# Neighbourhood attention and gated DeltaNet in one layer: keys, queries and values moved ahead of the gates, and the inverse's merges in a pool of their own

## The chip, the cores and the metric

The kernel runs on one core of one Trainium2 chip. The metric is the device time of one execution in microseconds (us). Before the change three runs gave 906.75, 904.99 and 906.35, a median of 906.35 us. The engines are called as in the profile: PE is TensorE (matrix products), PEld its weight load, DVE VectorE, ACT ScalarE, POOL GpSimd and SP SyncE, which issues nearly all DMAs. Each works through its own instructions in order.

## The reference

One layer mixes 1024 latent tokens (width 1024) and reads 256 context tokens. One input projection feeds two groups of heads; both are gated, joined and projected back:

```
h  = rmsnorm(x, g_pre) * (1 + scale) + shift          # modulated by c; hc for the context
na_q, na_k, na_v, na_z, g_qkv, g_z, g_b, g_a = split(h @ w_in)
o_na = neighborhood_attention(na_q, na_k, na_v, na_kc, na_vc, rpb)   # 8 heads of 64
q, k, v = gdn_qkv(g_qkv, conv_w)                       # short conv + silu, l2norm, rope; 4 heads of 128
...
a     = where(pos[:, None] > pos[None, :], (k * beta) @ k.T * decay, 0)
t_inv = inverse(eye + a)                               # one triangular inverse per chunk and direction
u, w  = t_inv @ (v * beta), t_inv @ (k * beta * exp(gc))
scan over chunks: v_new = u - w @ state; o = q_dec @ state + qk @ v_new; state = ...
...
y   = concat(o_na * silu(na_z), rmsnorm(o_g) * silu(g_z)) @ w_out
out = x + gate * rmsnorm(y, g_post)
```

DeltaNet runs in both directions. The kernel takes chunks of 128 tokens, so that there are ten blocks of 128 x 128 per head and direction (eight latent, two of context) whose triangular inverse is wanted.

## The kernel before

Five stages follow one another. **Setup and phase 0** load the modulation, form `h` and `hc` as pairs of a high and a low part (`hh`, `hl`), and make the first products. **Phase 2** runs over the four DeltaNet heads: per head the convolved projections of q and k, the front of the previous head (`delta_front`, which makes the triangular matrices `pm` and writes them to `pm_dram`), v, the token-wise work of q and k. **Phase a2** finishes the inverses. **Phase b** is neighbourhood attention (NA) with the scans of the DeltaNet heads woven in. **Phase 4** is the output projection.

Each product of float32 accuracy is three products: high by high, low by high, high by low (L460, L464, L465). Projections that nothing needs before phase b (NA's keys, queries, values and gates, and the gates of DeltaNet heads 1 to 3) are given out in steps by one generator, `projections` (L778). Phase 2 takes one step at each letter `p` of a string:

```
for c in "RVppTppUB":
    step(h, c)
    next(blocks, None)
```

That is four steps per head, sixteen in all. What is left of the generator is used up in phase a2. A step is one gate half (24 products of 512 columns), one block of keys or queries (24 of 512, or of 256 for the context), or values of two token tiles. `na_proj` writes keys and queries to `qk_dram` through `qk_out`; `gate_proj` writes gates to `z_dram`.

**The inverse** of a 128 x 128 block goes in two steps. The 32 x 32 diagonal blocks are inverted by substitution on DVE (`inv_blocks`, L1003 and L1006), in three groups: merge 0 needs group 0, merge 1 groups 0 and 1, merge 2 group 1, merge 3 group 2. Groups 0 and 1 run within phase 2, group 2 in phase a2 (generator `blocks`). The results go to `yd`. Then `inv_merge` (L1014), once per head, builds the 64 x 64 and then the 128 x 128 inverse from them: `vd` is the inverted diagonal blocks, loaded back, `ld` their transposes, `pmf` the head's `pm` matrices (two loads of 640 KB), `tz` the first products (PSUM), `zt` their copy in SBUF, `tu` the second products, which DVE scales by -1 into `tm` or `xo`; `tz2`, `z2`, `tu2` are the same at 64 x 64. The finished `tm` goes to `tm_dram`. The diagonal blocks are copied into `tm` and `xo` by twelve ACT copies. The trace prints `tz2` and `tu2` as `tz` and `tu`, without the head's number.

In phase a2 two generators, `blocks` and `merges`, are advanced beside the remaining projection steps, by a credit each. A Tile scheduler with a timeline of its own then sets the order of the instructions on every engine, by dependences and priority (`high_priority`); the merges run at a raised priority. The PSUM pool of these stages has three tags: `ta` (3 banks), `tb` (2) and `pj` (3).

## Time and profile before

| | |
|---|---|
| median of three runs | 906.35 us |
| profiled execution | 904.01 us, its span 902.3 us |
| mean granted PE clock | 0.963 |
| busy PE / DVE / ACT / POOL | 848.5 / 537.6 / 416.2 / 369.6 us |
| convolutions end (last key product of head 3) | 447.7 us |
| first merge product / first product of attention | 468.6 / 554.2 us |
| last stretch, the output projection, from about | 800 us |

The page gives busy time by engine, then forty slices of the span (each digit is tenths busy, for `PEclk` tenths of the full clock), then queues, the chain that ended last, and groups of instructions. A row of a timeline reads: start, length, engine, line, operation, output <- inputs, shape, count, and in brackets the idle time ahead of it with what ended it. A row of waits reads: engine, waiting tile and line, what it waited for, total us, times, longest. A row of DMA issues ends with the time from issue to landing. A row of a table of stretches reads: from:to, length, busy us (instructions) of PE, PEld, DVE, ACT and POOL, granted clock, share of the DMA engines, GB/s.

### The profile page before, as it was taken

How to read it: one execution, taken by the hardware profiler on the slowest of the kernel's cores; microseconds unless marked ns; L12 is line 12 of the kernel's file. 1: busy time of each engine (PE TensorE's matmuls, PEld its weight loads, DVE VectorE, ACT ScalarE, POOL GpSimd, SP SyncE). 2: the span in 40 equal slices, each digit the busy share in tenths (PEclk: the TensorE clock that was granted, in tenths of full speed). 3: DMA queues.
4: the chain of work that ended last, by engine and by line, in shares of the span. 5: the costliest groups of instructions: out<-in, count | busy, mean ns of one | idle time of the engine just before them, and what ended most of it. 6: DMA issues, size and time to landing. Idle time of an engine off the chain costs nothing.

```text
span 902.3 us, 16602 instructions
## 1 busy us (share of the span) xinstructions
PE 848.5 (94%) x6082; PEld 708.7 (79%) x6082; DVE 537.6 (60%) x1179; ACT 416.2 (46%) x1165; POOL 369.6 (41%) x431
## 2 busy tenths in 40 slices
PE   6999999999999989998998998999999988998996
PEld 4688887887788767787887877888887876887785
DVE  3463454456545699689428634677777775662442
ACT  5262525545645445652334444555545656532310
POOL 1432322614543532455241124568557569423210
PEclk9999999999999989999998985999999998999898
DMA  9786432346355534733799699949387152132351
GB/s 343 257 290 228 150 107 74 114 157 199 89 198 185 138 122 151 216 99 112 249 265 265 219 281 413 267 117 296 141 208 272 48 183 76 47 117 94 108 183 60
DMA packets 95176, 160.98 MB, mean 178 GB/s; under 512 B 28581, under 2 KB 55542, under 8 KB 92918
## 3 DMA queue, kind: packets, MB, share of 16 engines
q1 hardware_dynamic: 87606, 146.25, 51.2%
q10 hardware_dynamic: 7488, 13.67, 4.9%
q8 instruction: 48, 0.79, 0.4%
q14 instruction: 34, 0.28, 0.1%
HBM read 110.82 MB, written 52.42 MB: 181 GB/s over the span
## 4 chain that ended last, share of the span: by engine, by line
PE 64%; DVE 13%; DMA 9%; ACT 5%; issue 4%; POOL 2%; SPq 2%; ACTq 0%; DVEq 0%; POOLq 0%
PE py L1218 3%; PE py L1219 3%; PE py L1220 3%; DVE tb L1003 3%; PE pl L688 2%; DVE vb L1006 2%; PE po L715 2%; PE pl L697 2%; PE pz L464 2%; PE pc L684 2%; PE pz L460 2%; PE pz L465 2%; PE po L710 2%; PE pa L1138 2%; PE pa L1144 2%
## 5 line engine op out<-in xcount | busy, mean ns | idle before, releaser
L676 POOL TENSOR_TENSOR gm<-gt,mk 128x288 f32<-128x288 f32 (+1 forms) x64 | 64.3, 1009 | 36.0 <-DVE nm L693 35.9
L1125 POOL TENSOR_SCALAR kd<-kt,kd 128x128 f32<-128x128 f32 x72 | 43.4, 606 | 35.3 <-PE pa L1144 33.7
L694 ACT ACTIVATE pt<-pt,nm 128x288 f32<-128x288 f32 (+1 forms) x64 | 36.7, 574 | 35.7 <-DVE nm L693 35.5
L945 ACT ACTIVATE em<-em,gc 128x128 f32<-128x128 f32 x80 | 25.5, 391 | 38.2 <-DMA em<-gc_dram 32.3
L693 DVE CUSTOM_DVE_ANT_0 pt<-pl,gm,mi 128x288 f32<-128x288 f32 (+1 forms) x64 | 36.1, 564 | 11.5 <-PE pl L688 4.9
L699 DVE COPY tl<-pl 96x384 f32<-96x384 f32 (+1 forms) x64 | 35.3, 551 | 10.2 <-PE pl L697 9.9
L692 DVE TENSOR_REDUCE mi<-pc 128x1 f32<-128x256 f32 x64 | 26.8, 420 | 22.0 <-PE pc L684 21.1
L464 PE MATMUL pz<-hl,wh_gz 128*128 128x512 f32 x96 | 38.6, 402 | 0.0
L460 PE MATMUL pz<-hh,wh_gz 128*128 128x512 f32 x96 | 38.4, 400 | 0.0
L465 PE MATMUL pz<-hh,wl_gz 128*128 128x512 f32 x96 | 38.3, 399 | 0.0
L473 PE MATMUL pv<-wh_nv,hh 128*128 128x264 f32 x128 | 35.5, 295 | 2.5 <-ACT hh L262 1.7
L964 POOL TENSOR_SCALAR_AFFINE_SELECT qe<-qe 128x256 f32<-128x256 f32 x32 | 26.9, 840 | 25.8 <-DVE qe L963 25.8
L475 PE MATMUL pv<-wl_nv,hh 128*128 128x264 f32 x128 | 35.7, 286 | 1.5 <-POOL wl_nv L446 1.5
L474 PE MATMUL pv<-wh_nv,hl 128*128 128x264 f32 x128 | 36.5, 289 | 0.0
L1003 DVE TENSOR_TENSOR tb<-ab,vb 120x31 f32<-120x31 f32 (+15 forms) x62 | 32.1, 518 | 6.8 <-DMA ab<-ab_dram 5.1
L960 DVE SCALAR_TENSOR_TENSOR pm<-pk,beta,em 128x128 f32<-128x128 f32 x80 | 23.6, 343 | 19.9 <-PE pk L953 12.3
L697 PE MATMUL pl<-c,pt 128*96 128x128 f32 (+1 forms) x192 | 33.7, 285 | 1.4 <-ACT pt L694 1.2
L812 DVE SCALAR_TENSOR_TENSOR acc_v<-xp_v,cols,acc_v 128x1282 f32<-128x1282 f32 x16 | 27.5, 1719 | 9.0 <-ACT acc_v L810 8.9
L1138 PE MATMUL pa<-y,tm 128*128 128x128 f32 x144 | 29.1, 287 | 2.8 <-DVE y L1134 2.2
L1266 ACT ACTIVATE finv<-py 128x512 f32<-128x512 f32 x16 | 9.5, 599 | 46.8 <-PE py L1220 28.3
L1128 POOL TENSOR_SCALAR vb<-v,beta 128x128 f32<-128x128 f32 x40 | 24.2, 606 | 16.7 <-DVE y L1134 10.6
L704 ACT COPY tcx<-pc 128x256 f32<-128x256 f32 x64 | 23.8, 372 | 15.3 <-PE pc L702 15.1
(438 smaller groups left out, 2928.8 us busy)
## 6 DMA issues: line engine op xcount, KB each, us to landing
wada<-in_w_ada SPq DMA_DIRECT2D x16, 512.0 KB, 9.1
em<-gc_dram SPq DMA_DIRECT2D x20, 256.0 KB, 4.6
pm_dram<-pm SPq DMA_DIRECT2D x20, 256.0 KB, 3.3
pmf<-pm_dram SPq DMA_DIRECT2D x8, 640.0 KB, 8.0
tm_dram<-tm SPq DMA_DIRECT2D x8, 640.0 KB, 7.0
kk<-qk_dram SPq DMA_DIRECT2D x16, 320.0 KB, 7.9
tm<-tm_dram SPq DMA_DIRECT2D x4, 1280.0 KB
kq_dram<-kq SPq DMA_DIRECT2D x4, 1152.0 KB
```

The costliest lines, as they stand in the source:

```text
L460: r = nc.tensor.matmul(ps, wh, xh, start=(k == 0), stop=False)
L464: nc.tensor.matmul(ps, wh, xl, start=False, stop=False)
L465: nc.tensor.matmul(ps, wl, xh, start=False, stop=(k == KC - 1))
L474: nc.tensor.matmul(ps, xl, wh, start=False, stop=False)
L475: nc.tensor.matmul(ps, xh, wl, start=False, stop=(k == KC - 1))
L676: nc.gpsimd.tensor_tensor(gm[:, :n].rearrange("p (n c r) -> p n c r", c=nco, r=4), gv, mk[:, mo:mo + n].rearrange("p (n c r) -> p n c r", ...
L693: nc.vector.tensor_tensor_reduce(pt[:, :n], pl[:, :n], gm[:, :n], -1.0, mi, ALU.add, ALU.min, nm)
L694: nc.scalar.activation(pt[:, :n], pt[:, :n], AF.Exp, bias=nm, scale=-1.0, accum_out=sums[:, ct, hh, 0:1])
L697: nc.tensor.transpose(pl[:m, rc * P:(rc + 1) * P], pt[:, rc * m:(rc + 1) * m], self.ident)
L1003: nc.vector.tensor_tensor(t3, bc(ab[:, 0:m, m:m + 1], [r, m, n]), bc(vb[:, m:m + 1, m:], [r, m, n]), ALU.mult)
L1125: nc.gpsimd.tensor_scalar(kd, kt_[:, t, :], self.kd[:, h, d, t:t + 1], None, ALU.mult)
L1138: nc.tensor.matmul(pa, tm[:, d, t, :], y, start=True, stop=True)
```

## The change

It has four parts.

1. The order of the projections. Before: the gates of DeltaNet heads 1 to 3, then NA pair 1 (keys, queries, gate), the values in five steps, pairs 2 and 3 with their gates. After: pair 1 (three blocks of keys in three steps, both blocks of queries in one step), the values in four steps of up to three tiles, pairs 2 and 3; then all six gates. Keys, queries and values make sixteen steps, so that all of them are taken in phase 2 and the twelve gate steps are left for phase a2.
2. `inv_merge` takes its `pmf` tiles from one pair in a pool of its own (`pmf`, two tiles, both used by every head), instead of tiles that alternate between two places; `vd` has one buffer instead of two, `tm` four instead of three. The products `tz` and `tz2` use PSUM tag `ta` for heads 0 and 1 and `tb` for heads 2 and 3. `vd` is loaded ahead of `pmf`.
3. In the source, the copies into `tm` and `xo` stand behind the evictions `zt`.
4. `phase_a2` advances `merges` three times (priority 200) and `blocks` twice per projection step, and NA's first loads (`na_load` of pair 0) no longer wait for the merges.

```diff
@@ -525,16 +525,16 @@
         nc.sync.dma_start(self.qk_dram[1, rows, c0:c0 + n], lo.bitcast(F32))
 
 
-    def na_proj(self, ap, ps, pairs):
-        for p in pairs:
-            for i in range(2):
-                w = self.load_w(self.wp, 512 * i + P * p, P, f"n{'qk'[i]}{p}")
-                for gr in (2, 0, 1)[1 - i:]:
-                    pq = ps.tile([P, 512], F32, name=f"p{'qk'[i]}{p}_{gr}", tag="pj", bufs=3)
-                    self.mm_qk(pq, w, i, gr)
-                    self.qk_out(p, i, gr, pq)
+    def na_proj(self, ps, p):
+        for i in (1, 0):
+            w = self.load_w(self.wp, 512 * i + P * p, P, f"n{'qk'[i]}{p}")
+            for gr in (2, 0, 1)[1 - i:]:
+                pq = ps.tile([P, 512], F32, name=f"p{'qk'[i]}{p}_{gr}", tag="pj", bufs=3)
+                self.mm_qk(pq, w, i, gr)
+                self.qk_out(p, i, gr, pq)
+                if i:
                     yield
-            yield from self.gate_proj(ap, ps, p, 1536 + P * p)
+        yield
 
 
     def gate_proj(self, ap, ps, j, c0, w=None):
@@ -724,7 +724,7 @@
             rope = cv.tile([P, 1536], F32, name="rope")
             nc.sync.dma_start(rope, I["rope"])
             self.ssq = self.cp.tile([P, 4, 8], F32, name="ssq")
-            self.fill, self.ready = self.projections(cv), []
+            self.fill = self.projections(cv)
             kq, conv, toks = {}, {}, {}
 
             def step(h, c):
@@ -776,15 +776,15 @@
 
 
     def projections(self, pool):
-        for h in range(1, 4):
-            yield from self.gate_proj(pool, self.ps, 4 + h, 3584 + P * h)
-        yield from self.na_proj(pool, self.ps, [1])
-        w = self.load_w(self.wp, [(1024, 264)], 264, "nv0", halves=4)
-        for t in range(2, 12, 2):
-            self.values(pool, w, 0, [t % 10, t % 10 + 1])
-            yield
-        self.ready.append(True)
-        yield from self.na_proj(pool, self.ps, [2, 3])
+        for p in range(1, 4):
+            yield from self.na_proj(self.ps, p)
+            if p == 1:
+                w = self.load_w(self.wp, [(1024, 264)], 264, "nv0", halves=4)
+                for ts in ((2, 3), (4, 5, 6), (7, 8, 9), (0, 1)):
+                    self.values(pool, w, 0, ts)
+                    yield
+        for j, c0 in [(4 + h, 3584 + P * h) for h in range(1, 4)] + [(p, 1536 + P * p) for p in range(1, 4)]:
+            yield from self.gate_proj(pool, self.ps, j, c0)
 
 
     def conv(self, cv, ps, chunk, tag, has_ctx):
@@ -1013,18 +1013,19 @@
 
     def inv_merge(self, g3, ps, h):
         nc = self.nc
-        pm = []
-        for d in range(2):
-            pool, tag = (g3, f"pm{d}") if h % 2 else (self.pf, f"kk{d}")
-            pm.append(pool.tile([P, 10, P], F32, name=f"pmf{h}_{d}", tag=tag))
-            nc.sync.dma_start(pm[d], self.pm_dram[h][:, d])
-        vd = g3.tile([P, 2, 10, 32], F32, name=f"vd{h}", tag="vd", bufs=2)
+
+        ta, na = ("ta", 3) if h < 2 else ("tb", 2)
+        vd = g3.tile([P, 2, 10, 32], F32, name=f"vd{h}", tag="vd", bufs=1)
         ld = g3.tile([P, 2, 10, 32], F32, name=f"ld{h}", tag="ld", bufs=1)
+        zt = g3.tile([P, 2, 10, 32], F32, name=f"zt{h}", tag="zt", bufs=1)
+        pm = [g3.tile([P, 10, P], F32, name=f"pmf{h}_{d}", tag="pmf", bufs=2) for d in range(2)]
         for b in range(4):
             g, i = divmod(8 * h + 2 * b, 12)
             nc.sync.dma_start(vd[32 * b:32 * b + 32].rearrange("p d t i -> p (d t) i"),
                               self.yd[g][10 * i:10 * i + 20].rearrange("t j i -> j t i"))
-        tm = [g3.tile([P, 10, P], F32, name=f"tm{h}_{d}", tag="tm", bufs=3) for d in range(2)]
+        for d in range(2):
+            nc.sync.dma_start(pm[d], self.pm_dram[h][:, d])
+        tm = [g3.tile([P, 10, P], F32, name=f"tm{h}_{d}", tag="tm", bufs=4) for d in range(2)]
 
         xo = g3.tile([P, 10, 64], F32, name=f"xo{h}", tag="xo", bufs=1)
         for w in tm:
@@ -1032,16 +1033,8 @@
         nc.gpsimd.memset(xo, 0.0)
         yield
         nc.vector.transpose(ld.rearrange("p d t c -> p (d t c)"), vd.rearrange("p d t c -> p (d t c)"))
-        for b in range(4):
-            sl = slice(32 * b, 32 * b + 32)
-            cp = nc.scalar.copy
-            cp(tm[0][sl, :, sl], vd[sl, 0])
-            cp(tm[1][sl, :, sl], ld[sl, 1])
-            cs = slice(32 * (b % 2), 32 * (b % 2) + 32)
-            nc.scalar.copy(xo[sl, :, cs], ld[sl, 0] if b < 2 else vd[sl, 1])
-        zt = g3.tile([P, 2, 10, 32], F32, name=f"zt{h}", tag="zt", bufs=1)
         for d in range(2):
-            pz = ps.tile([P, 10, 32], F32, name=f"tz{h}_{d}", tag="ta", bufs=3)
+            pz = ps.tile([P, 10, 32], F32, name=f"tz{h}_{d}", tag=ta, bufs=na)
             for t in range(10):
                 for b in (0, 2):
                     s1, s2 = slice(32 * b, 32 * b + 32), slice(32 * b + 32, 32 * b + 64)
@@ -1050,6 +1043,12 @@
             for b in (0, 2):
                 s2 = slice(32 * b + 32, 32 * b + 64)
                 nc.scalar.copy(zt[s2, d], pz[s2])
+        for b in range(4):
+            sl = slice(32 * b, 32 * b + 32)
+            cs = slice(32 * (b % 2), 32 * (b % 2) + 32)
+            nc.scalar.copy(xo[sl, :, cs], ld[sl, 0] if b < 2 else vd[sl, 1])
+            nc.scalar.copy(tm[0][sl, :, sl], vd[sl, 0])
+            nc.scalar.copy(tm[1][sl, :, sl], ld[sl, 1])
         yield
 
         for d in range(2):
@@ -1070,7 +1069,7 @@
         A, B = slice(0, 64), slice(64, 128)
         parts = [(d, t0, 5) for d in range(2) for t0 in (0, 5)]
         for d, t0, n in parts:
-            pz = ps.tile([P, 8, 64], F32, name=f"tz2{h}_{d}{t0}", tag="ta", bufs=3)
+            pz = ps.tile([P, 8, 64], F32, name=f"tz2{h}_{d}{t0}", tag=ta, bufs=na)
             for t in range(n):
                 lo = xo[A, t0 + t, :] if d == 0 else tm[1][A, t0 + t, A]
                 nc.tensor.matmul(pz[B, t, :], pm[d][A, t0 + t, B], lo, start=True, stop=True, tile_position=(0, 64))
@@ -1276,48 +1275,32 @@
     def phase_a2(self):
         tc, ps = self.tc, self.ps
         with tc.tile_pool(name="a2", bufs=1, side="right", reuse_waits="tile") as ap:
-            ready = self.ready
-            buf = lambda nm, tag, n: self.pf.tile([P, n], F32, name=f"{nm}_{tag}", tag=tag)
-
             def blocks():
-                vv = buf("ab", "vv", 2 * S)
-                yield from self.inv_groups((2,), lambda nm, n: buf("tb2", "qh0", n) if n < S else vv[:, :S] if "ab" in nm
-                                           else vv[:, S:])
+                vv = self.pf.tile([P, 2 * S], F32, name="vv_inv", tag="vv")
+                yield from self.inv_groups((2,), lambda nm, n: self.pf.tile([P, n], F32, name=nm, tag="qh0") if n < S
+                                           else vv[:, :S] if "ab" in nm else vv[:, S:])
                 self.mk = self.pf.tile([P, MTOT], mybir.dt.bfloat16, name="mk")
                 self.load(self.mk, self.I["masks"])
-                while len(ready) < 4:
-                    yield
                 self.na_pairs = {0: self.na_load(None, 0)}
-                yield
 
             def merges():
                 for h in range(4):
                     while (8 * h + 7) // 12 not in self.yd:
                         yield
                     yield from self.inv_merge(ap, ps, h)
-                    ready.append(h)
-                    yield
-
-            pr, gens = self.fill, (blocks(), merges())
-            credit = [0.0, 0.0]
-            first = True
-            for _ in range(3):
-                next(pr)
-            for _ in pr:
-                for i, (g, r) in enumerate(zip(gens, (3, 3))):
-                    credit[i] += r
-                    while credit[i] > 0:
-                        if i:
-                            with tc.high_priority(offset=200):
-                                next(g, None)
-                        elif first:
-                            first = False
-                            with tc.high_priority(offset=300):
+
+            gens = [(merges(), 3, 200), (blocks(), 2, 0)]
+            with tc.high_priority(offset=300):
+                next(gens[1][0])
+            for _ in self.fill:
+                for g, n, p in gens:
+                    for _ in range(n):
+                        if p:
+                            with tc.high_priority(offset=p):
                                 next(g, None)
                         else:
                             next(g, None)
-                        credit[i] -= 1
-            for g in gens:
+            for g, *_ in gens[::-1]:
                 for _ in g:
                     pass
 
```

The order of instructions is set by the scheduler, so the diff tells little of it. Three places follow.

**PE, between merge 1 and merge 2.** `tz2_0` and `tz2_1` are the first products of merge 2, `tz21` and `tu21` the second stage of merge 1, `pz3` a gate projection of NA pair 3 and `wh_gz3`, `wl_gz3` its weights. Before:

```order
L1076 MATMUL tz21_15_4909<-tm1_1_4707,pmf1_1_4698 64x64 x5
L1048 MATMUL tz2_0_5021<-ld2_4996,pmf2_0_4991 32x32 x20
L1048 MATMUL tz2_1_5044<-ld2_4996,pmf2_1_4993 32x32 x14
L1082 MATMUL tu21_05_4930<-tm1_0_4706,z21_4887 64x64 x5
L1048 MATMUL tz2_1_5044<-ld2_4996,pmf2_1_4993 32x32 x5
L1084 MATMUL tu21_15_4931<-z21_4887,xo1_4708 64x64 x5
L1048 MATMUL tz2_1_5044<-ld2_4996,pmf2_1_4993 32x32
L460 MATMUL pz3_0_5644<-hh_112,wh_gz3_4_5639 128x512
L464 MATMUL pz3_0_5644<-hl_113,wh_gz3_4_5639 128x512
L465 MATMUL pz3_0_5644<-hh_112,wl_gz3_4_5640 128x512
```

and now:

```order
L1075 MATMUL tz21_10_4872<-tm1_1_4672,pmf1_1_4664 64x64 x5
L1075 MATMUL tz21_15_4879<-tm1_1_4672,pmf1_1_4664 64x64 x5
L1083 MATMUL tu21_10_4928<-z21_4857,xo1_4673 64x64 x5
L1081 MATMUL tu21_05_4941<-tm1_0_4671,z21_4857 64x64 x5
L1083 MATMUL tu21_15_4942<-z21_4857,xo1_4673 64x64 x5
L1041 MATMUL tz2_0_4975<-ld2_4958,pmf2_0_4960 32x32 x20
L1041 MATMUL tz2_1_4998<-ld2_4958,pmf2_1_4961 32x32 x20
L1061 MATMUL tu2_0_5086<-vd2_4957,zt2_4959 32x32
L1061 MATMUL tu2_0_5086<-zt2_4959,vd2_4957 32x32
```

Before, projections stand between the products of merge 1 and 2 and their successors; now the products of one merge follow on those of the last, and the last projection stands ahead of merge 1's `tu1_1`. In both orders the first product of attention stands behind the last of merge 3. Up to the last key product of head 3 the new order has 431 projection products of 512 columns, 72 of 256 and 240 of the values, against 353, 48 and 240. From there to the first merge product it has 62 gate products, against 90 of all kinds; and behind the first merge product 82, against 157.

**ACT, merge 2.** `zt2` are the evictions of the first products, `tm2` and `xo2` the copies, `z22` the evictions of the second stage. Before:

```order
L1077 COPY z21_4887<-tz21_15_4909 64x320
L1052 COPY zt2_5020<-tz2_0_5021 32x320 x2
L1052 COPY zt2_5020<-tz2_1_5044 32x320 x2
L1041 COPY xo2_5003<-ld2_4996 32x10x32 x2
L1041 COPY xo2_5003<-vd2_4995 32x10x32 x2
L547 ACTIVATE st_z30_5669<-pz3_0_5644 128x512
L1039 COPY tm2_1_5002<-ld2_4996 32x10x32 x4
```

and now:

```order
L1050 COPY tm2_0_4968<-vd2_4957 32x10x32 x4
L1049 COPY xo2_4970<-vd2_4957 32x10x32 x2
L1049 COPY xo2_4970<-ld2_4958 32x10x32
L1051 COPY tm2_1_4969<-ld2_4958 32x10x32
L1049 COPY xo2_4970<-ld2_4958 32x10x32
L1051 COPY tm2_1_4969<-ld2_4958 32x10x32 x3
L1045 COPY zt2_4959<-tz2_0_4975 32x320 x2
L1045 COPY zt2_4959<-tz2_1_4998 32x320 x2
L1076 COPY z22_5154<-tz22_00_5155 64x320
```

Before, eight of the twelve copies stand behind the evictions (the other four, of `tm2_0`, a few rows further ahead); now all twelve stand ahead of them. It is the same in merges 0 and 3; in merge 1 eight stand ahead.

**SP, around merge 3.** `pmf3` and `vd3` are the loads of merge 3, `yd2` the write of group 2's inverse, `tm_dram2` and `tm_dram1` the writes of merges 2 and 1. Before:

```order
L1020 DMA pmf3_0_5293<-pm_dram3_76 128x1280
L524 DMA qk_dram_93<-sh_k31_5626 128x512
L525 DMA qk_dram_93<-sl_k31_5627 128x512
L1012 DMA yd2_4987<-ab_vv_4368 80x1024
L153 DMA qh0_0_5269<-qk_dram_93 64x1024 x2
L1025 DMA vd3_5297<-yd2_4987 32x20x32
L1020 DMA pmf3_1_5295<-pm_dram3_76 128x1280
L1025 DMA vd3_5297<-yd2_4987 32x20x32 x3
L1090 DMA tm_dram1_86<-tm1_0_4706 128x1280
```

and now:

```order
L1089 DMA tm_dram1_86<-tm1_1_4672 128x1280
L153 DMA tm0_5783<-tm_dram0_85 128x2560
L153 DMA v0_5781<-vt_dram0_81 128x1280
L153 DMA kt0_5782<-kt_dram0_77 128x1280
L153 DMA kq0_5780<-kq_dram0_69 128x2304
L1165 DMA zg0_6611<-z_dram_95 128x1024
L1027 DMA pmf3_0_5333<-pm_dram3_76 128x1280
L1027 DMA pmf3_1_5334<-pm_dram3_76 128x1280
L1012 DMA yd2_5258<-vv_inv_4372 80x1024
L153 DMA qh0_0_5265<-qk_dram_93 64x1024 x2
L1089 DMA tm_dram2_87<-tm2_0_4968 128x1280
L1089 DMA tm_dram2_87<-tm2_1_4969 128x1280
L1024 DMA vd3_5330<-yd2_5258 32x20x32 x4
```

Before, the loads of merge 3 stood ahead of the writes of merge 1; now `pmf3` and `yd2` stand behind those of merge 1, and `vd3` behind those of merge 2. The load for group 2's inverse (`vv_inv`) stands behind the masks, both `kk0_0` and `ql0_0` loads and one of `kk0_1`, where it stood ahead of all of them.

## The prediction

> **What bounds the kernel now.** I read the page first (busy shares, the forty slices), then the table of stretches, then the waits of TensorE in the two stretches that the change touches, then the timelines of PE, ACT, DVE and SP there.
>
> ```profile
> PE 848.5 (94%) x6082; PEld 708.7 (79%) x6082; DVE 537.6 (60%) x1179; ACT 416.2 (46%) x1165; POOL 369.6 (41%) x431
> PE   6999999999999989998998998999999988998996
> PEclk9999999999999989999998985999999998999898
> ```
>
> PE is busy for 94% of a span of 902.3 us, so work that is only moved from one place on PE to another gains nothing by itself. A gain needs PE time that is idle, or runs at a low clock, where the work arrives, and no new idle time where it leaves. The clock row has one deep place, the 5 in slice 25. That is the end of the merges.
>
> ```profile
> 153.70:298.40 144.70, 144.23 (x746) 118.51 (x744) 75.44 (x113) 76.50 (x196) 65.69 (x66) 1.00 0.49 156
> 298.40:382.20 83.80, 78.01 (x396) 63.33 (x395) 71.19 (x123) 40.90 (x106) 33.51 (x35) 0.96 0.51 153
> 382.20:447.70 65.50, 59.74 (x399) 54.34 (x398) 50.90 (x99) 25.77 (x77) 29.54 (x22) 0.97 0.49 147
> 447.70:468.50 20.80, 20.80 (x91) 16.59 (x89) 6.41 (x16) 6.84 (x15) 9.03 (x12) 1.00 0.97 267
> 468.50:554.20 85.70, 77.41 (x1278) 65.73 (x1277) 48.20 (x112) 39.48 (x88) 17.91 (x19) 0.83 0.90 280
> 520.00:540.00 20.00, 17.99 (x316) 15.43 (x316) 6.62 (x13) 10.09 (x23) 4.05 (x5) 0.81 0.98 280
> 540.00:560.00 20.00, 16.27 (x225) 15.18 (x224) 8.37 (x20) 8.18 (x23) 8.12 (x11) 0.50 1.01 414
> 446.69 1.02 PE L955 MATMUL pk<-kq 128*128 128x256 f32 x4
> 468.56 1.45 PE L1048 MATMUL tz<-ld,pmf 32*32 32x32 f32 x80
> 492.64 1.45 PE L1048 MATMUL tz<-ld,pmf 32*32 32x32 f32 x80
> 554.23 0.58 PE L684 MATMUL pc<-kk,qh 128*128 128x256 f32 x1
> ```
>
> In the stretches each row has the length, then busy time of PE, weight load, DVE, ACT and POOL, the clock and the DMA share. The convolutions run to 447.7, where the last key product of head 3 ends (call it X). Then 20.8 us of projections cover the loads of merge 0, whose first product starts at 468.56; merge 1 starts at 492.64, and attention starts at 554.23, the moment the merges are done. From X to there it is 106.5 us. PE's idle time up to X is 0.47 + 5.79 + 5.76 = 12.0 us. In the merges it is 8.3 us, and the clock of 0.83 takes more; where little fill is left among them, it is 0.81 and then 0.50.
>
> ```profile
> PE tp L834 <- ACT sq L840: 4.9, 2, 4.5
> PE vtp L751 <- ACT vs L753: 3.9, 2, 3.2
> PE tz L1076 <- ACT tm L1039: 2.5, 1, 2.5
> PE tu L1062 <- ACT zt L1052: 2.4, 2, 2.2
> PE tu L1082 <- ACT z L1077: 2.0, 1, 2.0
> ```
>
> The first two rows are waits before X, the other three after it (total, times, longest). Before X two single stalls, 4.5 and 3.2 us, make most of the loss: PE stands behind ACT, which itself stands behind the taps and the inverse on DVE. After X PE waits for the links of the merge's own chain: product, eviction, product, scaling, product, eviction. With projections between the links these waits are short.
>
> **The change part by part.** *Projections moved ahead of X.* Sixteen steps are taken from the generator during the convolutions, before and after. Counted from the order of PE up to X, the changed program has 78 more products of width 512 and 24 more of width 256 there, since its sixteen steps hold all keys, queries and values and no gate.
>
> ```profile
> 153.69 0.40 PE L460 MATMUL pz<-hh,wh_gz 128*128 128x512 f32 x1
> 164.65 0.39 PE L465 MATMUL pz<-hh,wl_gz 128*128 128x512 f32 x1
> 437.42 0.28 PE L460 MATMUL pk<-chh,wh_nk 128*128 128x256 f32 x1
> 439.63 0.28 PE L464 MATMUL pk<-chl,wh_nk 128*128 128x256 f32 x1
> ```
>
> These are the first and last of 48 gate products (47 steps in 10.96 us, 0.233 each) and of a run of 20 context products (19 steps in 2.21 us, 0.116 each). So X moves back by 78 x 0.233 + 24 x 0.116 = 18.2 + 2.8 = 21.0 us if nothing is hidden. What is recovered, r, is bounded by zero below and by the whole loss above: 12.0 us idle, and at most 78.01 x 0.04 + 59.74 x 0.03 = 4.9 us of clock, so 16.9. The 4.5 us stall stands behind the same instructions in both orders, so I leave it; the 3.2 us one has more products ahead of it now, and loses some 2; the small ones and the clock give perhaps 3. I take r = 5.
>
> *Fill taken from the merges.* Behind the first merge product the old order has 157 fill products, spread over merges 0, 1 and 2. The new one has 82, all gone within merge 0 and the start of merge 1. Work that was cover there is worth its length only where PE was the limit; where the chain of the merge is the limit, its removal shortens nothing. So I rebuild the stretch from X to attention link by link.
>
> ```profile
> 536.24 0.86 ACT L1052 COPY zt<-tz 32x320 f32<-32x320 f32 x2 [2.24 <-PE tz L1048]
> 542.29 0.49 DVE L1067 TENSOR_SCALAR tm<-tu 32x320 f32<-32x320 f32 x1
> 548.19 0.48 DVE L1067 TENSOR_SCALAR tm<-tu 32x320 f32<-32x320 f32 x1 [0.95 <-POOL tm L1031]
> 554.33 0.49 DVE L1087 TENSOR_SCALAR tm<-tu 64x320 f32<-64x320 f32 x1 [0.79 <-PE tu L1084]
> POOL tm L1031 <- DMA tm_dram<-tm: 10.4, 4, 5.5
> L1020 SPq DMA_DIRECT2D pmf<-pm_dram x8: 320/480/625, 457.7 to 518.0; - x8
> DMA to landing us min/median/max: 8.0/8.0/8.0
> 518.47 2.02 SPq L1025 DMA_DIRECT2D vd<-yd  x3
> DMA to landing us min/median/max: 4.2/4.8/6.4
> 528.66 0.84 DVE L1034 STREAM_TRANSPOSE ld<-vd 128x640 f32<-128x640 f32 x1 [0.37 <-ACT tm L1039]
> L1038 ACT COPY tm<-vd x16: 443/456/459, 466.3 to 530.4; 32x320 f32<-32x320 f32 x16
> ```
>
> The first landing row is that of `pmf`, the second that of `vd`. Merge 3 is the old kernel's unfilled merge. From its first `zt` eviction to its last scaling it takes 554.82 - 536.24 = 18.6 us, of which 548.19 - 542.78 = 5.4 are a wait for a `tm` buffer that was still being written out. The fourth `tm` buffer removes that wait, so the link chain is 13.2 us, 14.7 with the 1.45 of `tz` ahead of it. The second product `tz2` is done about 3.6 before the end, 11.1 from the start.
>
> *One set of `pmf` tiles.* Before, even and odd heads had tiles of their own, and all eight loads were issued by 518.0, long ahead of their use. Now the load of merge h+1 waits until the `tz2` of merge h has read the tiles, and on SP it holds what stands behind it: the write of group 2's inverse behind `pmf3`, and `vd3` behind the writes of `tm2`.
>
> With these: `tz0` at X + 20.9 as before, since its loads stand in the same place behind the last write of head 3 and only 62 gate products (14.5 us) are left ahead of it, so some 6 us of PE go idle. First round: the old 492.64 - 468.56 = 24.1, plus the 8.0 of a reload that is no longer ahead, less 1 for less PE queueing: 31. Second round: 11.1 to the end of `tz2`, 0.5 to issue, 8.0 to land, 0.4 to start: 20. Third: 14.7 for the whole of merge 2, 2.0 to issue the four `vd3` loads, 4.8 to land, 0.8 for the transpose: 22.3. Last: 14.7. In all 20.9 + 31 + 20 + 22.3 + 14.7 = 108.9 us from X to attention, against 106.5. The bounds: 97, if one reload and half of another hide; 125, if the twelve copies of 0.456 (5.5 us), which the scheduler puts ahead of the `zt` evictions on ACT in merges 0, 2 and 3 although the source now has them behind, fall on the chain each time. I take the middle, as the row with the 8.0 us landings is the firm one.
>
> The Trainium skill, in "Trainium Kernel Development and Optimization", section "Best Practices", has a rule against this part: double-buffer, so that DMA overlaps with compute. If the tiles could have stayed two deep, the rounds would lose the two reloads and the stretch would be 108.9 - 16.5 = 92.4; the trace agrees so far that the old loads had all been issued by 518.0 and no PE wait names them.
>
> The skill's "TensorE: Matmul & The Clock Gate", section "Part 1: The HAM clock gate", says the clock halves after an idle window of about 3.4 us. The longest PE wait listed for the old merges is 2.5 us and the clock was 0.50 all the same, so the row is the harsher of the two; by either the reload gaps of 8 us leave the new merges at half clock, which the 14.7 us chain already holds.
>
> *NA's first loads, the masks, and group 2.* The first NA loads no longer wait for the merges; they stand ahead of the load for the inverse of group 2 on SP.
>
> ```profile
> 465.29 0.37 SPq L980 DMA_DIRECT2D ab_vv<-ab_dram  x1
> 472.26 0.20 DVE L1003 TENSOR_TENSOR tb_qh<-ab_vv 80x31 f32<-80x31 f32 x1 [3.96 <-DMA ab_vv<-ab_dram]
> ```
>
> That inverse started at X + 24.6, and only merge 3 needs its result. Its block can slip by the length of five or six loads, some 10 us, before it meets `tz3`, which this sum puts at X + 94. I cost it at nothing; it is in the upper bound. Attention itself is unchanged: it starts when the last merge ends, in both orders.
>
> *The sum.* Against the profiled execution's 904.0 us: 904.0 + 21.0 - 5 + (108.9 - 106.5) = 922.4. That run is 2.3 us under the median of the runs shown; I forecast 922.
>
> **The rivals.** *Hidden fill (faster).* All of the loss before X goes, r = 16.9, and the merges take their short bound, 97: 904.0 + 21.0 - 16.9 - 9.5 = 898.6. It decides once r plus what the merges gain exceeds 21.0 + 1.8 = 22.8. For it speaks that the stalls before X are of the kind more PE work fills; against it that PE was at 1.00 and 99.7% busy for 144.7 of these 294 us, and that the loss sits in two stalls.
>
> *No change.* r = 12 with merges of 97.5: 904.0 + 21.0 - 12 - 9 = 904. It needs nearly as much.
>
> *A new wait (worse).* The change doesn't do what it says on ACT: in three merges the copies run ahead of the evictions, 3 x 5.5 = 16.5 us, so that the stretch is 125 and the time 904.0 + 21.0 - 5 + 18.5 = 938.5. For it speaks the order; against it that the copies need only `vd`, which often lands before `pmf`.
>
> **How the numbers follow.** My forecast 0.65, faster 0.16, no change 0.06, worse 0.13. A change of 0.2% (1.8 us) is about what a measurement of this kernel tells from none. Slower is 0.65 + 0.13 = 0.78. The forecast's own range is 910 to 933 (r from 2 to 12, the stretch from 104 to 116); with a part of the cases on both sides it is 902 to 939.
>
> **What would show it.** Right, if in the new profile the last key product ends near 464, `tz0` starts 21 us later with a gap in front of it, PE's busy share between the first merge product and attention falls below 0.7 at a clock near 0.5, the waits of PE there name `pmf`, and `tz1`, `tz2`, `tz3` stand 20 us or more apart. Wrong, if X moves by less than 10 us, or if the stretch from X to attention is under 100 us: then the merges were bound by the projections on PE and not by their own chain.

## The result

The changed kernel took 919.42 us (median of four, 915.72 to 924.68), the kernel before 905.67 (median of four, 903.87 to 906.75) beside it. The ratio is 1.0161, with a 95% interval of 1.0127 to 1.0195: slower, by some 14 us or 1.6%. The profiled execution took 920.91 us, its span is 919.2.

The page of the changed kernel: busy shares, then PE and its clock in forty slices.

```profile
PE 851.7 (93%) x6082; PEld 713.3 (78%) x6082; DVE 537.7 (59%) x1179; ACT 416.6 (45%) x1165; POOL 373.6 (41%) x431
PE   6999999999999988989998856999999997999896
PEclk9999999999999999999999855999999999899899
```

PE does the same 6082 instructions in nearly the same busy time. The hole of the merges is deeper: the digits 8, 5, 6 in a row, where before no slice there stood under 8, and the clock is at 5 for two slices, where it was for one.

Three stretches of the kernel before: up to the last key product of head 3, from there to attention, and attention with everything behind it (from:to, length, busy time of PE, PEld, DVE, ACT and POOL, clock, DMA share, GB/s).

```profile
153.70:447.70 294.00, 281.99 (x1537) 236.18 (x1536) 197.54 (x335) 143.18 (x377) 128.74 (x123) 0.98 0.50 153
447.70:554.20 106.50, 98.21 (x1368) 82.31 (x1366) 54.61 (x128) 46.32 (x102) 26.94 (x31) 0.87 0.92 278
554.20:902.30 348.10, 323.84 (x2369) 274.92 (x2368) 212.59 (x599) 158.85 (x552) 172.03 (x224) 0.97 0.50 155
```

And the same three of the changed kernel.

```profile
153.70:468.80 315.10, 304.38 (x1646) 255.58 (x1645) 205.51 (x340) 150.10 (x388) 138.24 (x128) 0.98 0.49 155
468.80:572.40 103.60, 80.53 (x1266) 69.24 (x1265) 50.28 (x122) 41.68 (x95) 20.93 (x26) 0.73 0.92 286
572.40:919.20 346.80, 322.86 (x2369) 274.41 (x2368) 209.41 (x599) 158.52 (x552) 172.30 (x226) 0.97 0.48 144
```

Call the end of that key product X again. The first stretch got 21.1 us longer and PE's work in it 22.4. The second lost 17.7 us of PE work and became only 2.9 shorter. The third gained 1.3. Together 21.1 - 2.9 - 1.3 = 16.9, the difference of the spans. The first row starts at the same time in both kernels, not at the same product: at 153.7 us the changed kernel still had seven products of head 0's v to do (1.6 us) that the kernel before had behind it, so 20.8 of the 22.4 are the moved projections. PE's idle time ahead of X fell by only 1.3, from 12.0 to 10.7. So the work that arrived ahead of X cost about all its time, and the work that left the merges gave back a sixth of its time.

The waits of PE in the changed kernel, first up to about X, then behind it.

```profile
PE tp L834 <- ACT sq L840: 6.2, 2, 3.7
PE vtp L751 <- ACT vs L753: 4.1, 2, 3.0
```

```profile
PE tz L1041 <- DVE ld L1035: 10.5, 1, 10.5
PE tz L1075 <- DVE xo L1066: 2.9, 2, 2.4
PE tu L1061 <- ACT zt L1045: 2.9, 2, 1.4
```

The first two are the same waits as before the change, at 4.9 and 3.9 us then: in total neither became shorter. Behind X there is a new one of 10.5 us, ahead of merge 3. No such wait was among those of the kernel before, of which the longest was 2.5.

The merges of the changed kernel on PE, and what merge 3 waited for on DVE and SP.

```profile
467.75 1.02 PE L955 MATMUL pk<-kq 128*128 128x256 f32 x4
483.33 0.82 PE L1041 MATMUL tz<-ld,pmf 32*32 32x32 f32 x40
510.38 0.57 PE L1041 MATMUL tz<-ld,pmf 32*32 32x32 f32 x24
528.10 2.13 PE L1041 MATMUL tz<-ld,pmf 32*32 32x32 f32 x72 [1.51 <-issue]
556.28 2.34 PE L1041 MATMUL tz<-ld,pmf 32*32 32x32 f32 x80 [10.48 <-DVE ld L1035]
572.37 0.58 PE L684 MATMUL pc<-kk,qh 128*128 128x256 f32 x1
```

```profile
540.18 0.20 DVE L1006 TENSOR_TENSOR vv_inv<-vv_inv,tb 80x31 f32<-80x31 f32 x1
555.33 0.85 DVE L1035 STREAM_TRANSPOSE ld<-vd 128x640 f32<-128x640 f32 x1 [9.00 <-DMA vd<-yd]
```

```profile
539.95 2.45 SPq L1027 DMA_DIRECT2D pmf<-pm_dram  x2
542.50 0.38 SPq L1012 DMA_DIRECT2D yd<-vv_inv  x1
...
545.38 1.42 SPq L1089 DMA_DIRECT2D tm_dram<-tm  x2
548.28 4.51 SPq L1024 DMA_DIRECT2D vd<-yd  x4
```

The inverse of group 2 ends at 540.4, its write goes out at 542.5 behind `pmf3`, the loads of `vd3` from 548.3 behind the writes of merge 2, and the transpose starts at 555.3. The write landed at 548.2; SP had issued the writes of merge 2 by 546.8 and waited the last 1.4 us for that landing. Counted from X the merges start at 14.5, 41.6, 59.3 and 87.5, attention at 103.6.

### The profile page after: what moved, and what is told of

It reads as the page before. It is cut to its first block, busy times and chain, and to the rows that moved or that the text cites. A ratio compares the mean times of both kernels' runs of the same rounds, so it can differ in the third digit from the quotient of the medians.

```text
span 919.2 us, 16572 instructions
## 1 busy us (share of the span) xinstructions
PE 851.7 (93%) x6082; PEld 713.3 (78%) x6082; DVE 537.7 (59%) x1179; ACT 416.6 (45%) x1165; POOL 373.6 (41%) x431
## 5 line engine op out<-in xcount | busy, mean ns | idle before, releaser
L693 DVE CUSTOM_DVE_ANT_0 pt<-pl,gm,mi 128x288 f32<-128x288 f32 (+1 forms) x64 | 36.0, 563 | 10.4 <-PE pl L688 6.3
L812 DVE SCALAR_TENSOR_TENSOR acc_q<-xp_q,cols,acc_q 128x1024 f32<-128x1024 f32 x16 | 20.5, 1284 | 25.0 <-ACT acc_q L810 24.6
L1006 DVE TENSOR_TENSOR vb<-vb,tb 120x31 f32<-120x31 f32 (+15 forms) x62 | 31.9, 514 | 1.5
L1003 DVE TENSOR_TENSOR tb<-ab,vb 120x31 f32<-120x31 f32 (+15 forms) x62 | 28.2, 454 | 6.8 <-DMA ab<-ab_dram 5.1
L704 ACT COPY tcx<-pc 128x256 f32<-128x256 f32 x64 | 23.5, 369 | 16.7 <-PE pc L702 16.4
## 6 DMA issues: line engine op xcount, KB each, us to landing
tm<-tm_dram SPq DMA_DIRECT2D x4, 1280.0 KB, 10.9
```

What stands on the lines that cost most here:

```text
L693: nc.vector.tensor_tensor_reduce(pt[:, :n], pl[:, :n], gm[:, :n], -1.0, mi, ALU.add, ALU.min, nm)
L812: nc.vector.scalar_tensor_tensor(av, xp[:, s0 + tap:s0 + tap + 1282 - s0], wc(tap), av, ALU.mult, ALU.add)
```

## The experiments

Theories, by the letters of the expectations: **A**, the moved projections cost their time where they arrive, and each merge is bound by its own chain with the reloads of `pmf`; **B**, the order of the projections is neutral and the new pool of the merges costs the time; **C**, merge 3 waits for group 2; **D**, a chain of about 100 us through group 2 sets attention after X. S and Q came later, for what holds up merge 3.

In the table that follows, "X" is the end of head 3's last key product, then come the starts of merge 1 to 3 and of attention after X, "rest" is from attention to the end; all of the profiled execution. "Ahead" is the number of projection products (keys, queries, values and gates) that stand ahead of X in PE's order, counted from the start of the kernel. "Ratio" is to the kernel before, with its interval.

| run | ahead | X | merge 1, 2, 3 after X | attention after X | rest | median | ratio |
|---|---|---|---|---|---|---|---|
| before | 1097 | 447.7 | 44.9, 68.5, 85.8 | 106.5 | 348.1 | 904 to 906 | |
| the change | 1199 | 468.8 | 41.6, 59.3, 87.5 | 103.6 | 346.8 | 919.42 | 1.0161 (1.0127 to 1.0195) |
| e1, order alone | 1199 | 468.4 | 39.4, 56.8, 90.4 | 105.7 | 349.9 | 922.98 | 1.0205 (1.0165 to 1.0245) |
| e2, merges alone | 1097 | 446.5 | 47.4, 79.4, 96.9 | 116.9 | 355.0 | 921.64 | 1.0213 (1.0162 to 1.0264) |
| e3, `pmf` in two places | 1199 | 468.0 | 37.2, 59.2, 92.1 | 108.5 | 345.7 | 921.88 | 1.0191 (1.0153 to 1.0229) |
| e4, no wait for group 2 | 1199 | 466.1 | 42.7, 59.1, 81.4 | 96.6 | 350.2 | 916.92 | 1.0140 (1.0102 to 1.0177) |
| e5, before, two steps later | 1027 | 437.3 | 51.9, 71.2, 98.3 | 115.7 | 352.3 | 908.46 | 1.0048 (1.0025 to 1.0070) |
| e6, before, four later | 937 | 430.0 | 51.7, 76.9, 101.8 | 128.9 | 352.8 | 913.39 | 1.0108 (1.0083 to 1.0133) |
| e7, the change, four later | 1093 | 452.8 | 51.9, 83.3, 100.5 | 121.4 | 342.7 | 919.18 | 1.0173 (1.0137 to 1.0210) |
| e8, group 2's load first | 1199 | 466.8 | 43.0, 60.0, 88.7 | 104.8 | 345.1 | 922.39 | 1.0198 (1.0157 to 1.0238) |
| e9, before, steps ahead of T | 1064 | 441.2 | 50.8, 74.6, 93.3 | 115.5 | 346.2 | 905.05 | 1.0000 (0.9981 to 1.0019) |
| e10, before, four `tm` | 1097 | 447.8 | 48.8, 70.2, 86.6 | 103.1 | 357.4 | 911.22 | 1.0071 (1.0043 to 1.0099) |
| e11, merge 3's loads first | 1199 | 467.5 | 44.8, 62.1, 89.3 | 105.4 | 352.5 | 923.91 | 1.0216 (1.0186 to 1.0245) |
| e12, scan loads behind | 1199 | 467.7 | 43.5, 61.9, 77.9 | 94.2 | 355.4 | 918.41 | 1.0143 (1.0086 to 1.0200) |

**e1, the order alone.** The kernel before with `projections` and `na_proj` of the change.

```diff
-        for h in range(1, 4):
-            yield from self.gate_proj(pool, self.ps, 4 + h, 3584 + P * h)
-        yield from self.na_proj(pool, self.ps, [1])
...
+        for p in range(1, 4):
+            yield from self.na_proj(self.ps, p)
...
+        for j, c0 in [(4 + h, 3584 + P * h) for h in range(1, 4)] + [(p, 1536 + P * p) for p in range(1, 4)]:
+            yield from self.gate_proj(pool, self.ps, j, c0)
```

> The kernel before with the changed order of the projections alone; merges, pool and credits as before. Theory A (the moved projections cost their PE time where they arrive, and the merges, bound by their own chain, give only part of it back): the last key product of head 3 ends near 469 as in the changed kernel; the stretch from there to attention shrinks from 106.5 us to 92-100, since the loads of pmf stay ahead; time 911 to 919. Theory B (the order is neutral, the merge's new pool costs the 14 us): 904 to 907.

Measured: 922.98, over A's band too. The point X moved by 20.7, as expected, and B falls. But the stretch behind it did not shrink to 92 to 100: it is 105.7, with the old double `pmf`, the old pool and 15 us less of PE work in it (83.0 us busy against 98.2). Merges 1 and 2 do start earlier (39.4 and 56.8 against 44.9 and 68.5), merge 3 later. Its own rows on PE:

```profile
525.13 1.27 PE L1049 MATMUL tz<-ld,pmf 32*32 32x32 f32 x40
...
558.77 1.43 PE L1049 MATMUL tz<-ld,pmf 32*32 32x32 f32 x46 [8.72 <-DVE ld L1035]
```

Merge 3 waits for `ld`, the transpose of its diagonal blocks, without the single `pmf` tiles. A is right on the first stretch and not on the second.

**e2, the merges alone.** The changed kernel with the old `projections` and `na_proj`, the reverse of the diff above. Parts 2 to 4 of the change stay together in it.

> The changed kernel with the old order of the projections: only the merge pool, its PSUM tags, the copies and the credits are new. Theory A: the last key product ends near 448, and with 174 projection products behind the first merge product the reloads of pmf are mostly covered; the stretch to attention is 104 to 112 us, the time 903 to 911. Theory B: 918 to 921, as the whole change.

Measured: 921.64. A's 903 to 911 is missed as well. B's 918 to 921 is nearer, but e1 shows that the order is not neutral. The stretch is 116.9, ten more than before with the same projections in it, and the waits of PE in it name the reload:

```profile
PE tz L1040 <- DMA pmf<-pm_dram: 6.9, 4, 3.4
PE tz L1074 <- ACT z L1075: 2.2, 2, 1.7
```

The table adds a rest of 355.0, seven over the kernel before, to which I come back at the end. So each half of the change alone costs as much as both, for different reasons: the order moves X; the merges' parts lengthen a stretch that is still full of projections, with 6.9 of the 10.4 us as PE's wait for the reloads, and the rest adds 6.9. The PSUM tags, the place of the copies and the credits were not exchanged alone in any run.

**e3, `pmf` in two places.**

```diff
-        pm = [g3.tile([P, 10, P], F32, name=f"pmf{h}_{d}", tag="pmf", bufs=2) for d in range(2)]
+        pm = [g3.tile([P, 10, P], F32, name=f"pmf{h}_{d}", tag=f"pm{d}") if h % 2 else
+              self.pf.tile([P, 10, P], F32, name=f"pmf{h}_{d}", tag=f"kk{d}") for d in range(2)]
...
+                while len(done) < 3:
+                    yield
                 self.na_pairs = {0: self.na_load(None, 0)}
...
-            for g, *_ in gens[::-1]:
+            for g, *_ in gens:
```

The loop over `done` (the merges that are through) holds NA's first loads back until there are three, and the last line uses up the merges ahead of group 2's inverse at the end. So the edit is not the tiles alone.

> The changed kernel with pmf of even and odd heads in two places again, so that a merge's load is issued while the merge before it runs; NA's first key loads come after the merges for it. Theory A (reloads of 6 to 8 us stand on the chain between merges): tz1 and tz2 start 3 to 8 us earlier each, time 908 to 914. Theory C (merge 3 waits for the inverse of group 2 whatever the others do): merges 1 and 2 start earlier but merge 3 does not, attention starts within 3 us of 572, time 917 to 921.

Measured: 921.88, the interval overlapping the whole change's. Merge 1 starts 4.4 us earlier, merge 2 at the same place, merge 3 4.6 later. The PE waits behind X:

```profile
PE tz L1042 <- issue: 19.1, 2, 17.4
```

The 17.4 are ahead of merge 3 again: its `ld` is ready at 559.9, and it starts at 560.0. C comes nearest, though merge 2 did not start earlier, attention starts 4.5 us after C's 572, and the time is just over its band. What the earlier load gave back in merge 1 ran into the same wait. That wait is longer here than in the change, and in part by the edit itself: the load for group 2's inverse went out 27.0 us after X in place of 16.7, and the inverse ended 4.2 us later after X. So the run shows that merge 3's wait swallows the gain, and not what the single tiles would cost without it.

**e4, no wait for group 2.** Merge 3 reads group 0's diagonal blocks in place of group 2's, so head 3's inverse is that of other blocks; the amount of work is the same.

```diff
-            g, i = divmod(8 * h + 2 * b, 12)
+            g, i = divmod((8 * h + 2 * b) % 24, 12)
```

> The changed kernel in which merge 3 loads the diagonal blocks of group 0 in place of group 2 (so head 3's inverse is built from other data; the work is the same in size). Group 2 is still inverted, but nothing waits for it. Theory A: merge 3 still waits for its own pmf load behind merge 2's second stage, tz3 starts 549 to 552 in place of 556, time 912 to 916. Theory C: the 10.5 us wait ahead of tz3 goes wholly, tz3 starts right behind merge 2 at 546, time 908 to 911.

Measured: 916.92, just over A's band, with merge 3 at 547.5, between A's 549 to 552 and C's 546. After X merge 3 starts 6.1 us earlier, attention 7.0. What holds it now:

```profile
PE tz L1041 <- DMA pmf<-pm_dram: 5.4, 3, 4.5
```

So two things stand ahead of merge 3 one behind the other, the blocks of group 2 and then the reload of `pmf`. The profiled executions differ by 6.2 us (X 2.7 earlier, the stretch 7.0 shorter, the rest 3.4 longer), the medians by 2.5, and the intervals of the two ratios overlap: the gain is clear in the stretch and not in the whole.

**e5, e6, e7: fewer steps ahead of X.** Head 0 of the convolutions gives out two steps (e5) or none (e6) in place of four, in the kernel before; e7 is none in the changed kernel.

```diff
-                for c in "RVppTppUB":
+                for c in ("RVpTpUB" if h == 0 else "RVppTppUB"):
```

This is e5; e6 and e7 have `"RVTUB"` for head 0.

> The kernel before with two projection steps fewer in head 0 of the convolutions (14 in place of 16), which are left for the merges: 70 products fewer ahead of the last key product of head 3, and 34 of the projections now stand behind merge 3's first product. Theory D (from the last key product of head 3 a chain of about 100 us runs to attention, through group 2's load, its inverse on DVE, its write and load, and merge 3; PE work ahead of that point delays the chain, PE work behind it is covered by it): that point moves forward by 13 to 16 us, the stretch to attention grows by only 4 to 10 from 106.5, the time falls to 893 to 901. Theory A (each merge bound by its own chain wherever the fill stands, the fill between its links lengthens it): the stretch grows by as much as the point moves, time 903 to 908.

> The same with four steps fewer in head 0 (12 in place of 16): 160 products fewer ahead of the last key product of head 3. Theory D: that point moves forward by 27 to 35 us, but now PE itself is full behind it (98 us of work before, some 130 now), so the stretch is 130 to 138 and nothing more is won than with two steps; time 893 to 903. Theory A: 903 to 912.

> The changed kernel with four steps fewer in head 0, so that two blocks of keys or queries and all gates stand behind the last key product of head 3, 106 products fewer ahead of it. Theory D: that point moves back to 443 to 447, the group 2 chain sets attention some 104 to 112 us behind it, time 897 to 908. Theory A (single pmf tiles, reloads on the chain): the stretch is 115 to 120 as in the run with the merges alone, time 908 to 920.

Measured: 908.46, 913.39 and 919.18. D had promised a gain and is wrong as a description of the kernel before; A's upper ends, 908, 912 and 920, are nearer. X moves forward by 10.4 and 17.7 us in e5 and e6, less than the 13 to 16 and 27 to 35 expected, and the stretch grows by 9.2 and 22.4. Fewer projections ahead of X leave more idle time there: the waits of PE in e6 up to X are

```profile
PE vtp L751 <- ACT vs L753: 6.8, 2, 4.7
PE tp L834 <- ACT sq L840: 6.2, 3, 4.2
PE pv L475 <- DVE wl_nv L446: 2.3, 1, 2.3
```

16.5 us idle in all against 12.0. Behind X PE is nearly full in e6 (119.1 of 128.9 us busy), so work put there costs its time, and attention starts 4.7 us later than in the kernel before. In e5 the exchange is even: attention starts 1.3 us earlier, and the loss stands in the rest, which is 4.2 longer. In both, the first product of the scans starts later after attention than before (15.8 and 18.0 us in place of 6.5). In e7 the moved work is back behind X, and the stretch is 121.4 with 12.4 us of waits for `pmf` (6.9 in e2).

**e8, group 2's load first.** The masks and NA's first loads are queued behind that load.

```diff
+        self.inv_in = nc.sync.dma_start(ab[:n], self.ab_dram[120 * g:120 * g + n]).ins.name
...
+                self.gate = self.inv_in
                 self.load(self.mk, self.I["masks"])
                 self.na_pairs = {0: self.na_load(None, 0)}
+                self.gate = None
```

> The changed kernel in which the masks and NA's first loads are queued on SP behind the load for group 2's inverse; in the order that follows the write of that inverse also stands ahead of merge 3's pmf loads. Theory D (after the last key product of head 3 the chain group 2 load, inverse, write, load, merge 3 sets attention): the inverse starts about 24.5 us after that point in place of 27.5 and ends 3 us earlier, its write goes 2 us earlier, the stretch falls from 103.6 to 98-100, time 913 to 917. Theory A: no change, 917 to 922.

Measured: 922.39. The inverse started at 20.2 and ended at 63.5 after X, 8 us earlier than in the change, and its write went out then; merge 3 did not move (88.7). D in this form falls too: it is not the inverse on DVE that holds merge 3. The landing times of the tiles `yd`, which are the writes of the inverses and the loads from them, show one of 14.3 us:

```profile
DMA to landing us min/median/max: 2.6/4.7/14.3
```

That is the write of group 2, issued at 530.4 and landed at 544.6; the first load of `vd3` went out at 544.7.

**e9, steps ahead of T.** The kernel before with `"RVpppTpUB"` for every head.

> The kernel before with the four projection steps of each head placed three ahead of the token work T and one behind it, in place of two and two. If the stalls ahead of the last key product of head 3 (12.0 us idle) are gaps that any PE work given out ahead of them fills, idle there falls to about 5 us and the time to 897 to 901. If a stall hangs on DVE and ACT work that itself follows PE's own earlier product, more PE work ahead delays both alike and the idle time stays at 10 to 13 us: time 903 to 909.

Measured: 905.05, a ratio of 1.0000. Some 30 projection products also came to stand behind X that were ahead of it. Idle time ahead of X went from 12.0 to 9.9, and changed its place: `tp` nearly stopped waiting, `vtp` waits longer.

```profile
PE vtp L751 <- ACT vs L753: 5.4, 1, 5.4
PE pv L475 <- DVE wl_nv L446: 3.1, 1, 3.1
...
PE tp L834 <- ACT sq L840: 0.4, 1, 0.4
```

Here filling one gap opened another. In e1 and the whole change, with a hundred products more ahead of X, the idle time there was 10.9 and 10.7.

**e10, four `tm` tiles.**

```diff
-        vd = g3.tile([P, 2, 10, 32], F32, name=f"vd{h}", tag="vd", bufs=2)
+        vd = g3.tile([P, 2, 10, 32], F32, name=f"vd{h}", tag="vd", bufs=1)
-        tm = [g3.tile([P, 10, P], F32, name=f"tm{h}_{d}", tag="tm", bufs=3) for d in range(2)]
+        tm = [g3.tile([P, 10, P], F32, name=f"tm{h}_{d}", tag="tm", bufs=4) for d in range(2)]
```

> The kernel before with four tm tiles and one vd tile in the merges, the sizes of the change alone. Theory A: the 5.4 us that merge 3's scalings waited for a tm tile still being written out go, merge 3 takes 13 to 14 us in place of 18.6, the stretch falls from 106.5 to 101-103, time 899 to 902. Rival: the one vd tile makes vd of the next merge late by its landing of 4.8 us in each round and eats it, 903 to 908.

Measured: 911.22, over both bands. The stretch fell to 103.1, at the edge of what A said: merge 3 takes 16.5 us in place of 20.7. The rest rose by 9.3, and the sum is slower.

**e11, merge 3's loads first.** On top of e8, `vd3` is queued ahead of `pmf3`, and both ahead of the writes of merge 2's `tm`.

```diff
+            p = nc.sync.dma_start(pm[d], self.pm_dram[h][:, d])
+            if h == 3:
+                self.order(p, r.ins.name)
+        if h == 3:
+            for d in range(2):
+                self.order(nc.sync.dma_start(self.tm_dram[2][:, d], self.tm2[d]), p.ins.name)
...
+        if h == 2:
+            self.tm2 = tm
+            return
```

> The kernel of e8 (group 2's load first) in which on SP merge 3's vd loads stand ahead of its pmf loads, and both ahead of the writes of merge 2's tm. In e8 the inverse of group 2 was done 63.5 us after the last key product of head 3 and written at once, yet merge 3 started at 88.7, its vd loads issued behind those writes. Theory S (the queue order on SP, a load that waits behind a write that waits for the whole merge before): the vd loads go out when merge 2 has read its vd, some 70 us after that point, the pmf loads at 71-73 and land 8 later; merge 3 starts at 80 to 83, the stretch falls from 104.8 to 96-99, time 912 to 916 against e8's 922. Rival (the loads land late because the DMA queues are full there, whatever stands ahead): merge 3 still starts at 86 to 90, time 918 to 923.

Measured: 923.91, and merge 3 at 89.3: the rival, not S. It was the write that landed late, and the loads of `vd3` went out behind it. SP's queue in this run, then the wait of SP for that write, then the stretch from 530 to 540 (columns as above), then the landing times of the tiles `yd`:

```profile
533.42 0.63 SPq L1012 DMA_DIRECT2D yd<-vv_inv  x1
537.06 2.03 SPq L153 DMA_DIRECT2D qh<-qk_dram  x2
549.01 1.98 SPq L1024 DMA_DIRECT2D vd<-yd  x4
```

```profile
SPq L1024 <- DMA yd<-vv_inv: 9.8, 1, 9.8
```

```profile
530.00:540.00 10.00, 5.12 (x200) 4.72 (x195) 4.64 (x16) 3.49 (x8) 1.72 (x2) 0.50 1.01 363
```

```profile
DMA to landing us min/median/max: 2.3/3.9/15.5
```

The write of group 2's inverse, 0.3 MB, was issued at 533.4 and took 15.5 us to land, at a DMA share of 1.01; SP stood until 549.0. Just ahead of it, from 527 to 533, the four loads of the first scan and its gate had gone out.

**e12, the scan's loads behind.** On top of e11:

```diff
+            self.m3 = p.ins.name
...
-            if h or i >= 4:
-                self.gate = self.na_first
+            self.gate = self.na_first if h or i >= 4 else self.m3
             self.load(dst, src)
```

> The kernel of e11 in which the four loads of the first scan (tm0, v0, kt0, kq0, 3.8 MB, which went out at 527 to 533 just ahead of the write of group 2's inverse) stand behind merge 3's loads. In e11 that write took 15.5 us from issue to landing, at a DMA share of 1.01, and the vd loads waited 9.8 us for it. Theory Q (the DMA engines were full of the scan's loads, and the small write and merge 3's loads stood in their tail): the write lands within 6 us, vd goes out when merge 2 has read its vd, merge 3 starts 79 to 83 us after the last key product of head 3 in place of 89.3, the stretch is 95 to 99 in place of 105.4, attention starts near 564, time 912 to 918 against e11's 924 and the whole change's 919. Rival (the scan's loads are only moved on to where attention and the first scan wait for them): merge 3 starts early but the first products of attention and the scan wait, time 919 to 925.

Measured: 918.41. SP and PE of this run:

```profile
533.04 0.33 SPq L1012 DMA_DIRECT2D yd<-vv_inv  x1
533.42 1.20 SPq L153 DMA_DIRECT2D qh<-qk_dram  x2
537.76 1.98 SPq L1024 DMA_DIRECT2D vd<-yd  x4
```

```profile
545.58 1.28 PE L1047 MATMUL tz<-ld,pmf 32*32 32x32 f32 x40
561.86 0.58 PE L684 MATMUL pc<-kk,qh 128*128 128x256 f32 x1
```

`vd3` went out 4.7 us behind the write, 70 after X; merge 3 started 77.9 and attention 94.2 after X, 11.2 us earlier than in e11. Q is right on the mechanism: bulk loads of the next phase, issued into the same DMA engines, held up the small write that merge 3 hung on. With them behind merge 3's loads, that write landed in 4.7 us in place of 15.5. Neither e8 nor e11 could show a gain while those loads stood ahead; the last edit without the two others was not tried. On the time Q misses its band by 0.4: the rest is 355.4, 2.9 more than in e11 and 8.6 more than in the change. The rival, that the first scan would wait for the moved loads, is not seen: the first product of the scans starts 4.1 us after attention, in e11 4.2.

**The rest.** Nothing from attention on was edited (e12 moves four of its loads), and PE's busy time there is 319 to 328 us in all the runs, yet it takes from 342.7 to 357.4. The scheduler weaves attention and scans anew with nearly every edit ahead of them. Where it is long, in e10 and e12, PE waits there for the softmax and the scans' output:

```profile
PE pl L697 <- ACT pt L694: 8.4, 6, 4.7
PE pos L1152 <- DVE o L1160: 4.3, 3, 3.2
```

```profile
PE pl L697 <- ACT pt L694: 11.8, 11, 5.2
PE pos L1159 <- DVE o L1167: 4.5, 3, 3.4
```

(e10, then e12; the change has 4.6 and none.) The runs fall into groups by where the output projection starts. In e2, e4, e10, e11 and e12 its first product stands 252 to 260 us after attention, behind the last scans, and their rests are 350 to 357. In the other nine it stands 235 to 243 us after attention, in all but e7 with scans still to come, and their rests are 343 to 350, but for e5 and e6 with their late scans (352 and 353). Where two kernels have the same order of PE row for row from attention on, the rests differ by 1.7 us (e8 and the change) and 1.9 (e9, in all but a few rows, and the kernel before). That the later output projection is what makes those five 3 to 11 us longer than the change is read from this grouping; no run exchanged the weave alone.

No run beat the kernel before; e9 equals it.

## Why the prediction was right

The time was forecast at 922 within 902 to 939, and is 919.4. The main mechanism holds: the projections that moved ahead of X cost their length there (e1 has that alone, with X 20.7 us later), and the merges gave back little of it. That the total came so near is in part luck, since two of its terms were wrong by 5 us in opposite directions.

**The projections ahead of X.** The price, 21.0 us, was right: X moved by 21.1 in the change and by 20.7 in e1, and the moved projections are 20.8 us of PE's work. The term r = 5 was wrong. PE idled 10.7 us ahead of X in place of 12.0, and these 1.3 were lost again by the 1.6 us that the changed kernel was behind at 153.7. The step that failed is "the small ones and the clock give perhaps 3", with the 2 of the 3.2 us stall, which measures 3.0. In e9 a gap that was filled in one place opened at the next link of the same head; whether the gaps of the change stay for the same reason was not tested.

**The start of merge 0.** Predicted 20.9 after X with a gap of 6; measured 14.5, and with no gap. The last load of `vd0` landed 11.7 us after X, in the kernel before 19.6, so "its loads stand in the same place" was wrong by 6 us.

**The rounds.** Predicted 31, 20, 22.3 and 14.7; measured 27.1, 17.7, 28.2 and 16.1. In the first two the reload was overpriced. The row of 8.0 that the prediction called the firm one holds a single landing, and the one of the changed kernel holds two, of 4.1 us (merge 2) and 5.9 (merge 3):

```profile
DMA to landing us min/median/max: 4.1/5.0/5.9
```

Merge 1 started 4.7 us after its first reload was issued. That bears on the two sentences ahead that drew on the Trainium skill. The rule of "Trainium Kernel Development and Optimization", "Best Practices", to double-buffer, would have taken 16.5 us off this sum. In e3 merge 1 started 4.4 us earlier and the time did not fall, because another wait stood behind; since e3 also moved group 2's load, it doesn't price the rule alone. In e2 and e7, where projections keep PE busy among the merges, PE waits 6.9 and 12.4 us for those loads, so there the rule has a price. Of "TensorE: Matmul & The Clock Gate", "Part 1: The HAM clock gate", the forecast that the new merges stay at half clock held for merges 2 and 3: the clock was 0.50 from 527 us to attention, with PE's wait of 10.5 us in it (first row below). Over nearly all of the four merges it was 0.68.

```profile
550.00:560.00 10.00, 2.34 (x80) 2.24 (x80) 0.85 (x1) 5.91 (x14) 0.00 (x0) 0.50 0.95 268
485.00:573.00 88.00, 65.35 (x1150) 57.20 (x1143) 45.69 (x110) 32.72 (x74) 10.84 (x13) 0.68 0.92 291
```

**The third round** was too small by 5.9. The sum had 14.7 for merge 2, then 2.0 to issue `vd3`, 4.8 to land and 0.8 for the transpose. Merge 2 took 18.2, to its last scaling at 546.3; then 1.9 passed until the first load of `vd3`, issuing took 4.5, the transpose started 2.5 later and 1.0 after that the merge. So 3.5 us are merge 2's own, and 4.4 stand in the way to `vd3` and its issue, less 2.1 of a faster landing and start. "I cost it at nothing" was said of group 2's slip. The inverse did slip, but in e8 it came 8 us earlier and merge 3 stayed. What the sum left out is that the write of group 2 must land before `vd3` goes out, in DMA engines that were at a share of 1.03 from its issue to its landing. It took 5.7 us to land in the change, 14.3 in e8 and 15.5 in e11. Without that wait (e4) merge 3 starts 6.1 us earlier, and with the write landing early and `vd3` behind it at once (e12) 9.6.

**Attention after X.** 108.9 predicted, 103.6 measured, so 5.3 too long, against 5.1 too short ahead of X. The two cancel: 904.0 + 21.1 - 2.9 - 1.3 = 920.9 is the profiled run.

**The rivals.** "Hidden fill" did not happen, since X moved by the whole price. Its condition was stated rightly (r plus the gain of the merges over 22.8; here 0 + 2.9). "A new wait" priced the copies ahead of the evictions at 5.5 us a merge. They do stand on the chain, but with their tail alone: in merge 3 the first half of `tz` was done at 557.6, the last copy at 559.1, and the first eviction followed at 559.15; in merge 2 the delay is the same 1.6 us. Six of merge 3's twelve ran ahead of its first product, while PE waited. Merge 3 took 16.1 us from its first product to attention, 1.4 over the sum without them.

**The marks.** X near 464: 468.8. `tz0` 21 us behind with a gap: 14.5 without. PE under 0.7 behind the first merge product at a clock near 0.5: 65.4 of 88.0 us busy, which is 0.74, at a clock of 0.68 (the second row above). `tz1` to `tz3` 20 us or more apart: 27.1, 17.7, 28.2. The waits that should name `pmf` name `ld`.
